# A two-layer trunk: the second layer's output projection as seven half-size products

## The chip, the cores and the metric

The kernel runs on one core of one Trainium2 chip. The metric is the device time of one execution in microseconds (us); each kernel has several timed runs and one profiled execution.

## The reference, cut to what matters

`x` has 512 tokens by 1024 features in float32. The first layer is a pooling mixer, the second a latent attention with 16 heads of 128. Both end in an output projection of 2048 by 1024, and a final norm follows:

```python
def pool_layer(x, norm_g, w_in, w_group, scale, w_out):
    ...
    y = mixed * jax.nn.silu(z)
    return x + y @ w_out

def mla_layer(x, cos, sin, norm_g, w_in, q_norm_g, w_q_b, kv_norm_g, w_kv_b, w_out):
    ...
    o = causal_mla_attention(q_nope, q_rope, k_nope, k_rope, v)
    y = o.reshape(B, S, MLA_WIDTH) * jax.nn.silu(z)
    return x + y @ w_out

def reference(...):
    ...
    return rmsnorm(x, final_norm)
```

## The kernel before

Every float32 matmul is made of three: each operand is split into a high part (float32r, written by ScalarE, ACT) and a low part (the rest, written by VectorE, DVE, or now and then GpSimd, POOL), and `mm3` (L181) issues high x high, low x high and high x low. `strip` (L170) loads a piece of weights through five `raw` buffers and splits it into a pair of `w` tiles, of which four stand (two strips at a time). `halves` (L187) splits an activation. Work is traced in program order; a planner with its own cost model then sets the order of instructions on each engine and inserts the semaphores, but the final block (`finish`) keeps its written order. All plain DMAs go through the queue of SyncE (SP); DMAs that add into SBUF go through POOL's.

The first layer's output projection is done as seven products of half size (L581 to L722). `y` is cut into quarters: `a11` and `a12` are the first 256 tokens with the first and second 1024 of the contraction, `a21` and `a22` the last 256 tokens. Sums of quarters of `y` are made on DVE (`combine`, L628) and split (`split_tokens`, L632). Sums of quarters of the weights are made by DMA: `Summed.load` (L587) loads a quarter into four tiles of 512 KB by SP and then, with `add`, has POOL issue DMAs that add another quarter into the same tiles. `multiply` (L638) is one product: 2 token tiles x 8 contraction tiles x 3 = 48 matmuls of 128x512. `gather` (L657) adds a bank to the residual `xs`.

In the second layer heads run in the loop at L1103. Head h computes the scores of head h+1, transposes head h's probabilities (`transposes`, L1053; DVE writes `pt_lo`), and multiplies by the values (`values`, L1068, which also scales `y`). Heads 0 to 13 cover the softmax's latency with projections of later heads; heads 12 to 15 have blocks of the output projection as fill:

```python
fill = {12: [(0, 0)], 13: [(0, 1)], 14: [(1, 0), (1, 1)], 15: [(2, 0), (2, 1)]}
```

`OutProj` (L529) does this projection in the ordinary way: eight strips of 256 contraction rows, each for four token tiles and two halves of the columns, accumulated in eight banks: 16 x 4 x 2 x 3 = 384 matmuls of 128x512, the last six of them cut into twelve of 128x256. Each strip's weights and two heads of `y` are split on ACT and DVE. 36 matmuls run as fill, the rest after head 15 (L1136 to L1144). `finish` (L1193) does the last strip token tile by token tile, with squares, the power on POOL, the gain and the scaling, and eight output DMAs.

Of the kernel before, what the change touches and what calls it, by code (L numbers as in the profile page):

```python
# [11 lines left out]
F32 = mybir.dt.float32  # L12
# [5 lines left out]
P = 128  # L18
D = 1024
# [31 lines left out]
def trunk_kernel(  # L51
# [477 lines left out]
    class OutProj:  # L529
        def __init__(self, w, apart=None):  # L530
            self.w, self.acc, self.st, self.apart = w, {}, {}, apart

        def load(self, s, tile_of):
            (wv,) = strip([(w_rows(self.w, 2 * s, 2), 2, D)])
            ys = []
            for j in range(2):
                yh, yl = tile_of("h", j), tile_of("l", j)
                halves(y[:, 2 * s + j, :], yh, yl)
                ys.append((yh, yl))
            self.st[s] = (wv, ys)  # L540

        def strip(self, s):
            for j in range(2):
                for t in range(NT):
                    for n in range(2):
                        self.block(s, t, n, j)

        def block(self, s, t, n, j):
            wv, ys = self.st[s]
            if (t, n) not in self.acc:  # L550
                self.acc[t, n] = bank()
            mm3(
                self.acc[t, n],
                tuple(v[:, t * P : (t + 1) * P] for v in ys[j]),
                tuple(v[:, j, n * 512 : (n + 1) * 512] for v in wv),
                s == 0 and j == 0,
                j == 1 and s == (6 if self.apart == (t, n) else 7),
            )

        def columns(self, o, s, t, c):  # L560
            wv, ys = self.st[s]
            for j in range(2):
                mm3(
                    o,
                    tuple(v[:, t * P : (t + 1) * P] for v in ys[j]),
                    tuple(v[:, j, c] for v in wv),
                    j == 0,
                    j == 1,
                )

        def add(self, t, n):
            c = slice(n * 512, (n + 1) * 512)
            return dve.tensor_tensor(xs[:, t, c], self.acc[t, n], xs[:, t, c], ALU.add)

    w_out = pool_w_out[0]
    LEFT, RIGHT = slice(0, 512), slice(512, D)

    class Summed:  # L581


        def __init__(self, tiles):
            self.tiles = tiles
# [677 lines left out]
```

## Time and profile before

| what | value |
|---|---|
| median of 3 runs | 727.72 us (726.13 to 728.48) |
| the profiled execution's own time | 728.38 us |
| its span, first to last instruction | 726.6 us |
| mean granted TensorE clock over the span | 0.992 of full speed |

The span leaves out 1.78 us of the execution's own time. PE is TensorE's matmuls, PEld its weight loads. A matmul's listed duration is longer than its distance to the next one, since matmuls are pipelined: the distance between starts is what counts. Idle time in front of an instruction is shown with what released it.

### The profile page before, as it was taken

The page shows a single profiled execution, that of the slowest core. Times are in us where ns is not written, and L with a number is a line of the kernel's source. Part 1 is how long each engine was busy: PE and PEld are TensorE (multiplying, and loading weights), DVE is VectorE, ACT ScalarE, POOL GpSimd, SP SyncE. Part 2 cuts the span into 40 slices and gives each one's busy share as a digit, 9 for nine tenths or more (in the row PEclk, how much of TensorE's full clock was granted, in tenths as well). Part 3 has the DMA queues.
Part 4 walks back from the last instruction along what each step waited for, and adds up shares of the span by engine and source line. Part 5 has one row for each costly group of instructions (what it writes and reads, how often), then busy time and mean ns, then how long its engine had stood idle before and what let it go on. Part 6 is the DMA issues. An engine that isn't in the chain of part 4 may idle for free.

```text
span 726.6 us, 9988 instructions
## 1 busy us (share of the span) xinstructions
PE 712.1 (98%) x3571; PEld 607.1 (84%) x3571; DVE 417.6 (57%) x834; ACT 337.0 (46%) x739; POOL 116.9 (16%) x159
## 2 busy tenths in 40 slices
PE   7999999999999999999999999999999999999995
PEld 7988888888888887799888888888888988888884
DVE  5964453463577897742724212786876877733325
ACT  6452242242244466545723235575566565533314
POOL 5000000000001350145500023222033100000006
PEclk8999999999999999999999999999999999999998
DMA  8341331332365996135333523132142131113203
GB/s 260 109 142 60 115 115 60 115 112 62 116 189 111 243 179 132 53 109 153 103 102 83 142 74 94 52 81 63 44 113 66 37 96 59 59 59 116 95 7 115
DMA packets 65057, 74.38 MB, mean 102 GB/s; under 512 B 11760, under 2 KB 45680, under 8 KB 65008
## 3 DMA queue, kind: packets, MB, share of 16 engines
q1 hardware_dynamic: 60512, 65.16, 30.1%
q0 software_dynamic: 4352, 8.39, 6.6%
q8 instruction: 28, 0.46, 0.3%
q14 instruction: 21, 0.17, 0.1%
q10 hardware_dynamic: 144, 0.20, 0.1%
HBM read 67.44 MB, written 2.10 MB: 96 GB/s over the span
## 4 chain that ended last, share of the span: by engine, by line
PE 86%; DMA 4%; issue 3%; DVE 3%; POOL 2%; ACT 1%; SPq 0%; POOLq 0%; ACTq 0%
PE bank L185 26%; PE bank L183 26%; PE bank L184 26%; PE bank L1059 2%; PE bank L301 2%; DMA b_y<-in_pool_w_out 2%; PE bank L1022 1%; PE bank L1023 1%; DMA b_x<-in_pool_w_out 1%; POOL b_x L591 1%; DMA raw<-in_pool_w_in 1%; PE bank L1025 1%; PE bank L226 1%; ACT pm L1045 1%; DVE pm L1051 1%
## 5 line engine op out<-in xcount | busy, mean ns | idle before, releaser
L166 ACT ACTIVATE w_hi<-raw 128x512 fp32r<-128x512 f32 (+2 forms) x216 | 114.1, 580 | 153.3 <-PE bank L184 142.3
L167 DVE TENSOR_TENSOR w_lo<-raw,w_hi 128x512 fp32r<-128x512 f32 x148 | 96.8, 690 | 135.6 <-ACT w_hi L166 135.6
L183 PE MATMUL bank<-h_hi,w_hi 128*128 128x512 f32 x368 | 143.4, 390 | 0.0
L185 PE MATMUL bank<-h_lo,w_hi 128*128 128x512 f32 x368 | 143.2, 389 | 0.0
L184 PE MATMUL bank<-h_hi,w_lo 128*128 128x512 f32 x368 | 143.2, 389 | 0.0
L167 POOL TENSOR_TENSOR w_lo<-raw,w_hi 128x256 fp32r<-128x256 f32 (+2 forms) x68 | 61.3, 933 | 193.4 <-ACT w_hi L166 193.3
L185 PEld LDWEIGHTS bank<-h_lo,w_hi 128*128 128x128 f32 x368 | 69.1, 188 | 14.4
L183 PEld LDWEIGHTS bank<-h_hi,w_hi 128*128 128x128 f32 x368 | 69.1, 188 | 14.3
L184 PEld LDWEIGHTS bank<-h_hi,w_lo 128*128 128x128 f32 x368 | 69.1, 188 | 14.2
L185 PE MATMUL bank<-w_lo,h_hi 128*128 128x512 f32 (+1 forms) x176 | 64.2, 365 | 0.4 <-DVE w_lo L608 0.4
L183 PE MATMUL bank<-w_hi,h_hi 128*128 128x512 f32 (+1 forms) x176 | 64.6, 367 | 0.0
L184 PE MATMUL bank<-w_hi,h_lo 128*128 128x512 f32 (+1 forms) x176 | 64.1, 364 | 0.0
L183 PE MATMUL bank<-latT_hi,w_hi 128*128 128x512 f32 x104 | 42.3, 406 | 0.0
L185 PE MATMUL bank<-latT_lo,w_hi 128*128 128x512 f32 x104 | 40.7, 391 | 0.0
L184 PE MATMUL bank<-latT_hi,w_lo 128*128 128x512 f32 x104 | 40.6, 391 | 0.0
L1029 DVE CUSTOM_DVE_ANT_0 pm<-bank,mask 128x128 f32<-128x128 f32 (+2 forms) x64 | 30.6, 489 | 16.0 <-PE bank L185 11.0
L185 PEld LDWEIGHTS bank<-w_lo,h_hi 128*128 128x128 f32 x176 | 33.0, 188 | 5.3 <-DVE w_lo L608 0.8
L183 PEld LDWEIGHTS bank<-w_hi,h_hi 128*128 128x128 f32 x176 | 33.0, 188 | 4.4
L184 PEld LDWEIGHTS bank<-w_hi,h_lo 128*128 128x128 f32 x176 | 33.1, 188 | 4.3
L1045 ACT ACTIVATE pm<-pm,nm 128x128 f32<-128x128 f32 (+1 forms) x64 | 35.3, 557 | 2.4 <-DVE nm L1042 2.0
L188 ACT ACTIVATE pt_hi<-bank 128x512 fp32r<-128x512 f32 (+2 forms) x48 | 20.1, 491 | 23.3 <-PE bank L1059 23.3
L456 POOL MEMSET u<- 128x32 f32 x8 | 1.0, 125 | 178.9 <-DVE sums L468 106.1
(209 smaller groups left out, 1414.5 us busy)
## 6 DMA issues: line engine op xcount, KB each, us to landing
raw<-in_pool_w_in SPq DMA_DIRECT2D x64, 256.0 KB, 3.1
raw<-in_mla_w_in SPq DMA_DIRECT2D x32, 256.0 KB, 3.3
raw<-in_mla_w_out SPq DMA_DIRECT2D x32, 256.0 KB, 3.3
b_x<-in_pool_w_out POOLq DMA_DIRECT2D x12, 512.0 KB, 7.7
raw<-in_mla_w_q_b SPq DMA_DIRECT2D x36, 128.0 KB, 2.5
raw<-in_pool_w_group SPq DMA_DIRECT2D x16, 256.0 KB, 2.7
q_r<-stack SPq DMA_DIRECT2D x64, 64.0 KB, 2.0
raw<-in_mla_w_kv_b SPq DMA_DIRECT2D x16, 256.0 KB, 2.9
```

Of the source, the lines that this page charges most:

```text
L166: act.activation(hi, raw, AF.Copy)
L167: ins = eng.tensor_tensor(lo, raw, f32(hi), ALU.subtract)
L183: pe.matmul(o, a[0], b[0], start=start, stop=False, skip_group_check=more)
L184: pe.matmul(o, a[1], b[0], start=False, stop=False, skip_group_check=more)
L185: pe.matmul(o, a[0], b[1], start=False, stop=stop, skip_group_check=more)
L188: act.activation(hi, src, AF.Copy)
L226: pe.transpose(pt[:, i * P : (i + 1) * P], xn[:, k * P : (k + 1) * P], ident)
L301: pe.matmul(first[i][:, c], w0.views[0][a][:, k, i * P : (i + 1) * P], (h_hi, h_lo)[b][:, k, c], start=k == 0 and n == 0, stop=k == KD - 1 ...
L591: pool.dma_start(t, src, accum_op=ALU.add)
L1029: dve.tensor_tensor_reduce(out=pm[:, OFF[i] : OFF[i] + w], in0=o[:, :w], in1=mask[:, S - w :], scale=1.0, scalar=-3.0e38, op0=ALU.add, op1 ...
L1045: act.activation(v, v, AF.Exp, bias=nm[:, i : i + 1], scale=SCALE, accum_out=l[:, i : i + 1])
L1059: pe.transpose(b[:, n : n + P], pm[:, OFF[i] + j * P : OFF[i] + (j + 1) * P], ident)
```

## The change

The second layer's projection is done by the first layer's seven products, so 7 x 48 = 336 matmuls of 128x512 stand where 384 stood (the last twelve of them are cut into 24 of 128x256). `OutProj` goes away; `Summed`, `combine`, `split_tokens` and `multiply` become functions for both layers, with the first layer's calls and order as before.

The first product (`a11`, heads 0 to 7, with the upper left quarter of the weights) is the fill of heads 12 to 15, twelve matmuls in each. Between the heads stand also: the splits of `a11` (heads 12 and 13), the two strips of its weights, loading and adding the second product's weights (`x_sum`, now eight tiles of 256 KB that take over buffers of queries and keys), the differences `s1` and `s2` of three of the four pieces of `y`, and part of their splits. After head 15 the last piece is made, and the other six products follow. `y_sum` (four tiles of 512 KB) takes over the buffers of the probabilities. `finish` does the seventh product: token tiles 0 and 1 are normed during it, tile 2 behind it, and tile 3's left half is computed in two parts of 256 columns; `normed` multiplies by the row's factor and the gain in one DVE instruction, and the last output halves leave by SP's and ACT's queues.

```diff
...
+        def __init__(self, w, n):
+            self.w, self.n, self.tiles = w, n, []
+        def load(self, half, c, add=False, pieces=None):
+            for i in pieces or range(len(self.tiles)):
+                src = w_rows(self.w, half * 8 + self.n * i, self.n)[:, :, c]
                 if add:
+                    pool.dma_start(self.tiles[i], src, accum_op=ALU.add)
                 else:
+                    nc.sync.dma_start(self.tiles[i], src)
+        def strip(self, i, eng=dve):
             hi = wp.tile([P, W], F32R, name="w_hi", tag="w", bufs=WB)
             lo = wp.tile([P, W], F32R, name="w_lo", tag="w", bufs=WB)
             hv, lv = (t.rearrange("p (k c) -> p k c", k=4) for t in (hi, lo))
+            m = 4 // self.n
+            for j in range(m):
+                k = slice(self.n * j, self.n * (j + 1))
+                raw = self.tiles[m * i + j]
+                act.activation(hv[:, k, :], raw, AF.Copy)
+                eng.tensor_tensor(lv[:, k, :], raw, f32(hv[:, k, :]), ALU.subtract)
+            return hv, lv
+        def strips(self):
+            return [self.strip(i) for i in range(2)]
...
+    def part(o, wv, slot, q, t, start, stop, more, c=whole_row):
+        for k in range(4):
+            mm3(
+                o,
+                tuple(v[:, 4 * q + k, t * P : (t + 1) * P] for v in slot),
+                tuple(v[:, k, c] for v in wv),
+                start and k == 0,
+                stop and k == 3,
+                more=more,
+            )
+    def multiply(banks, strips, slot, start, then=None):
+        for q in range(2):
+            for t in range(2):
+                part(banks[t], strips[q], slot, q, t, start and q == 0, q == 1, not start)
+                if then and q == 1:
+                    then(t)
...
-    o2 = OutProj(mla_w_out[0], apart=(NT - 1, 1))
-    def y_late(half, j):
-        n = "qk"[j] + half
-        return ap.tile([P, S], F32R, name=n, tag=n, bufs=2)
+    w_out2 = mla_w_out[0]
+    a11, a12, a21, a22 = quarters()
+    x_sum, y_sum = Summed(w_out2, 1), Summed(w_out2, 2)
+    def slot_of(hi, lo):
+        return tuple(
+            home.tile([P, 8, 256], F32R, name=name, tag=tag, bufs=1)
+            for name, (home, tag) in (("a_hi", hi), ("a_lo", lo))
+        )
+    def sum_tiles(n):
+        for i in range(n):
+            tag = ("qh", "ql", "kh", "kl")[i]
+            x_sum.tiles.append(ap.tile([P, 1, S], F32, name="b_x", tag=tag, bufs=2))
     (k0, q0), (k1, q1), vs = projections(0)
     qr = {1: QRope(1)}
@@ -1099,13 +1073,22 @@
     for u in vs:
         u()
     units = projections(1)
-    fill = {12: [(0, 0)], 13: [(0, 1)], 14: [(1, 0), (1, 1)], 15: [(2, 0), (2, 1)]}
+    first_half, slots = {}, {}
     for h in range(H):
         p, odd = divmod(h, 2)
         g, t = divmod(h + 5, 4)
-        if h == min(fill):
-            o2.load(0, y_late)
+        if h == 12:
+            slots[1] = slot_of((lp, "t2"), (lp, "q_r"))
+            first_half[0] = columns_of(w_out2, 0, LEFT, 0)
+            split_tokens(a11, slots[1], (0, 1))
+            acc = [bank() for _ in range(2)]
+        if h == 13:
+            split_tokens(a11, slots[1], (2, 3))
         nxt = scores(h + 1) if h + 1 < H else None
+        if h in (13, 14):
+            sum_tiles(4)
+            x_sum.load(0, LEFT, pieces=range(4 * (h - 13), 4 * (h - 12)))
+            x_sum.load(0, RIGHT, add=True, pieces=range(4 * (h - 13), 4 * (h - 12)))
         if odd:
             ahead = projections(p + 2) if p + 2 < H // 2 else [[], [], []]
         transposes(sc[0])
@@ -1115,9 +1098,23 @@
             units[odd][0]()
         if units[odd]:
             units[odd][1]()
-        for i, (t_, n) in enumerate(fill.get(h, ())):
-            for j in range(2):
-                o2.block(0, t_, n, j)
+        if h >= 12:
+            q, t_ = divmod(h - 12, 2)
+            part(acc[t_], first_half[q], slots[1], q, t_, q == 0, q == 1, False)
+        if h == 14:
+            slots[0] = slot_of((lp, "latT_hi"), (wk, "q_r"))
+            s1 = lp.tile([P, 8, 256], F32, name="s1", tag="latT_lo", bufs=1)
+            s1 = [s1[:, 2 * i : 2 * i + 2, :] for i in range(4)]
+            s2 = [
+                lp.tile([P, 2, 256], F32, name="s2", tag=tag, bufs=1)
+                for tag in ("cosT", "sinT", "k_a", "k_b")
+            ]
+            combine(s1, a21, a22, ALU.subtract, range(3))
+            split_tokens(s1, slots[0], range(2))
+        if h == 15:
+            t1 = x_sum.strip(0)
+            split_tokens(s1, slots[0], (2,))
+            combine(s2, s1, a11, ALU.subtract, range(3))
         values(h)
         if g < 4 and t < 2:
             if t == 0:
@@ -1129,96 +1126,135 @@
             for u in units[2]:
                 u()
             units = ahead
+        if h == 13:
+            first_half[1] = columns_of(w_out2, 0, LEFT, 1)
         sc = nxt
+    combine(s1, a21, a22, ALU.subtract, (3,))
+    split_tokens(s1, slots[0], (3,))
+    y_sum.tiles = [
+        ap.tile([P, 2, S], F32, name="b_y", tag=tag, bufs=n)
+        for tag, n in (("pm", 2), ("pm", 2), ("pt_hi", 1), ("pt_lo", 1))
+    ]
+    y_sum.load(1, RIGHT)
+    both = [bank() for _ in range(2)]
+    t1 = [t1, x_sum.strip(1)]
+    x_sum.load(1, RIGHT, add=True)
+    multiply(both, t1, slots[0], True)
+    for t in range(2):
+        gather(t, LEFT, acc[t])
+    combine(s2, s1, a11, ALU.subtract, (3,))
+    split_tokens(s2, slots[1])
+    multiply(acc, x_sum.strips(), slots[1], False)
+    x_sum.load(1, LEFT, add=True)
+    for t in range(2):
+        gather(2 + t, RIGHT, both[t])
+    combine(s2, s2, a12, ALU.add)
+    split_tokens(s2, slots[0])
+    for t in range(2):
+        gather(t, RIGHT, acc[t], ALU.subtract)
+    multiply(both, y_sum.strips(), slots[0], False)
+    y_sum.load(0, RIGHT, add=True)
     g_fin = row(final_norm, D, "g_fin", tag="gain")
-    o2.load(1, y_late)
-    for n in range(2):
-        for j in range(2):
-            o2.block(0, 3, n, j)
-    o2.strip(1)
-    for s in range(2, 8):
-        o2.load(s, y_late)
-        if s < 7:
-            o2.strip(s)
+    s3 = [
+        v.rearrange("p (i k c) -> p i k c", i=2, k=2)[:, i]
+        for v in (xn_tile(), xn_tile())
+        for i in range(2)
+    ]
+    combine(s3, a11, a21, ALU.subtract)
+    split_tokens(s3, slots[1])
+    for t in range(2):
+        gather(t, RIGHT, both[t])
+    multiply(acc, y_sum.strips(), slots[1], False)
+    split_tokens(a12, slots[0])
+    last = [bank() for _ in range(2)]
+    multiply(last, [columns_of(w_out2, 1, LEFT, i) for i in range(2)], slots[0], True)
     o = [
         ap.tile([P, D], F32, name="o", tag=tag, bufs=n)
         for tag, n in (("pm", 2), ("pm", 2), ("pt_hi", 1), ("pt_lo", 1))
     ]
-    junk = lp.tile([P, 512], F32, name="junk", tag="t2", bufs=1)
+    junk = lp.tile([P, 512], F32, name="junk", tag="turned", bufs=1)
     ssq = {t: [] for t in range(NT)}
     rs = {}
...
+    def square(t, c):
         r = sm.tile([P, 1], F32, name="ssq", tag="ssq8", bufs=12)
+        act.activation(
+            junk[:, : c.stop - c.start], xs[:, t, c], AF.Square, scale=D**-0.5, accum_out=r
+        )
         ssq[t].append(r)
     def total(t):
         r = sm.tile([P, 1], F32, name="total")
         pool.tensor_scalar(r, ssq[t][0], EPS, None, ALU.add)
         for q in ssq[t][1:]:
             pool.tensor_tensor(r, r, q, ALU.add)
+        ssq[t] = [r]
+    def power(t):
         rs[t] = sm.tile([P, 1], F32, name="rs")
-        pool.tensor_tensor(rs[t], r, mhalf, ALU.pow)
-    def gained(eng, t, c):
-        eng.tensor_tensor(o[t][:, c], xs[:, t, c], g_fin[:, c], ALU.mult)
-    def scaled(eng, t, c, queue=nc.sync):
-        if eng is act:
-            act.activation(o[t][:, c], o[t][:, c], AF.Copy, scale=rs[t])
-        else:
-            eng.tensor_scalar(o[t][:, c], o[t][:, c], rs[t], None, ALU.mult)
+        pool.tensor_tensor(rs[t], ssq[t][1], ssq[t][0], ALU.add)
+        pool.tensor_tensor(rs[t], rs[t], mhalf, ALU.pow)
+    def send(t, c, queue=nc.sync):
         queue.dma_start(out[0, t * P : (t + 1) * P, c], o[t][:, c])
+    def normed(t, c):
+        dve.scalar_tensor_tensor(
+            o[t][:, c], xs[:, t, c], rs[t], g_fin[:, c], ALU.mult, ALU.mult
+        )
+        send(t, c)
+    def gained(t, c):
+        dve.tensor_tensor(o[t][:, c], xs[:, t, c], g_fin[:, c], ALU.mult)
+    def scaled(t, c, queue=nc.sync):
+        act.activation(o[t][:, c], o[t][:, c], AF.Copy, scale=rs[t])
+        send(t, c, queue)
+    for t in range(2):
+        gather(2 + t, RIGHT, acc[t], ALU.subtract)
+    split_tokens(a22, slots[1])
+    t4 = x_sum.strips()
     def finish():
...
+        for t in range(2):
+            square(t, RIGHT)
+            square(2 + t, RIGHT)
+        for t in range(2):
+            gather(t, LEFT, last[t])
             total(t)
-            if t == 1:
-                scaled(act, 0, lefts)
-                scaled(act, 0, rights)
-        scaled(act, 1, lefts)
-        block(3, 0)
-        o2.add(3, 0)
-        square(3, lefts)
-        gained(pool, 3, lefts)
-        scaled(dve, 1, rights)
-        columns(slice(512, 768))
-        square(3, slice(512, 768))
-        columns(slice(768, D))
-        square(3, slice(768, D), dve)
-        scaled(dve, 2, rights)
-        scaled(act, 2, lefts)
+            square(t, LEFT)
+            power(t)
+        for t in range(2):
+            part(acc[t], t4[0], slots[1], 0, t, False, False, True)
+            for c in (LEFT, RIGHT):
+                normed(t, c)
+        part(acc[0], t4[1], slots[1], 1, 0, False, True, True)
+        gather(2, LEFT, acc[0])
+        total(2)
+        square(2, LEFT)
+        gained(3, RIGHT)
+        c0, c1 = slice(0, 256), slice(256, 512)
+        part(acc[1][:, c0], t4[1], slots[1], 1, 1, False, True, True, c0)
+        power(2)
+        rest = bank()[:, c0]
+        part(rest, t4[1], slots[1], 1, 1, True, True, False, c1)
+        gather(3, LEFT, acc[1])
+        square(3, c0)
         total(3)
-        gained(dve, 3, rights)
-        scaled(dve, 3, slice(0, 640))
-        scaled(act, 3, slice(640, D), act)
+        normed(2, LEFT)
+        gather(3, c1, rest)
+        square(3, c1)
+        power(3)
+        normed(2, RIGHT)
+        scaled(3, RIGHT, act)
+        normed(3, LEFT)
     with tc.manual_schedule():
         finish()
```

## Rows read from the trace of the kernel before

**Rows 1.** The page: busy us (share of the span) and instructions of an engine.

```profile
...
PE 712.1 (98%) x3571; PEld 607.1 (84%) x3571; DVE 417.6 (57%) x834; ACT 337.0 (46%) x739; POOL 116.9 (16%) x159
```

**Rows 2.** Windows: stretch, length, busy us of each engine, PE clock, DMA share, GB/s.

```profile
...
600.00:640.10 40.10, 40.10 (x237) 35.14 (x236) 27.79 (x75) 22.65 (x63) 0.00 (x0) 1.00 0.17 53
640.10:718.50 78.40, 78.35 (x353) 64.92 (x351) 30.92 (x48) 25.92 (x51) 7.96 (x13) 1.00 0.22 71
234.50:311.00 76.50, 75.51 (x340) 62.04 (x340) 61.43 (x79) 43.89 (x62) 22.52 (x22) 1.00 0.72 150
...
234.30:245.20 10.90, 10.90 (x49) 9.01 (x48) 10.86 (x15) 6.33 (x8) 4.85 (x4) 1.00 1.00 259
```

**Rows 3.** Timeline of PE, the projection's end: start, duration, line, operation, operands.

```profile
...
709.38 0.39 PE L183 MATMUL bank<-w_hi,kh 128*128 128x512 f32 x1
...
716.63 0.39 PE L185 MATMUL bank<-w_lo,kh 128*128 128x512 f32 x1
716.86 0.28 PE L183 MATMUL bank<-w_hi,qh 128*128 128x256 f32 x1
...
718.17 0.28 PE L185 MATMUL bank<-w_lo,kh 128*128 128x256 f32 x1
```

**Rows 4.** Timeline of PE in the first layer's fifth product.

```profile
...
279.24 0.40 PE L184 MATMUL bank<-w_hi,h_lo 128*128 128x512 f32 x1
280.04 0.50 PE L185 MATMUL bank<-w_lo,h_hi 128*128 128x512 f32 x1 [0.41 <-DVE w_lo L608]
```

**Rows 5.** Timeline of DVE: splits and sums of pieces, several in a row.

```profile
...
235.70 2.35 DVE L608 TENSOR_TENSOR w_lo<-b_x,w_hi 128x1024 fp32r<-128x1024 f32 x2
...
266.52 1.29 DVE L189 TENSOR_TENSOR h_lo<-s,h_hi 128x512 fp32r<-128x512 f32 x2
...
643.76 2.49 DVE L167 TENSOR_TENSOR w_lo<-raw,w_hi 128x512 fp32r<-128x512 f32 x4
```

**Rows 6.** Timeline of PE and DVE at the last two heads.

```profile
...
634.42 1.18 PE L1059 MATMUL bank<-ident,pm 128*128 128x128 f32 x9
...
638.40 0.39 PE L183 MATMUL bank<-pt_hi,xn 128*128 128x512 f32 x1
...
633.62 1.28 DVE L1051 TENSOR_SCALAR pm<-pm,l 128x128 f32<-128x128 f32 x4
...
636.00 1.49 DVE L189 TENSOR_TENSOR pt_lo<-bank,pt_hi 128x512 fp32r<-128x512 f32 x3 [0.51 <-ACT pt_hi L188]
640.39 0.69 DVE L1082 TENSOR_TENSOR y<-bank,y 128x512 f32<-128x512 f32 x1 [2.90 <-PE bank L1081]
```

**Rows 7.** POOL's adding DMAs, first layer: timeline, tile b_x, queues at 244:254.

```profile
...
242.50 2.43 POOL L591 DMA_DIRECT2D b_x<-in_pool_w_out  x2 [2.62 <-DVE w_lo L608]
...
L591 POOL DMA_DIRECT2D b_x<-in_pool_w_out x12: 1194/1206/1524, 226.8 to 262.2; - x12
...
DMA to landing us min/median/max: 4.4/7.3/10.7
...
q0 software_dynamic: 1062, 2.04, 112.3%
```

**Rows 8.** Timelines of DVE, ACT, POOL in the tail; last, a first-layer norm.

```profile
...
718.87 0.75 DVE L1191 TENSOR_TENSOR xs<-bank,xs 128x256 f32<-128x256 f32 x2
...
719.40 0.42 ACT L1163 ACTIVATE junk<-xs 128x256 f32<-128x256 f32 x1
...
722.29 0.62 ACT L1183 ACTIVATE o<-o,rs 128x384 f32<-128x384 f32 x1 [1.77 <-POOL rs L1176]
...
720.72 0.89 POOL L1174 TENSOR_TENSOR total<-total,ssq 128x1 f32<-128x1 f32 x2
721.69 0.57 POOL L1176 TENSOR_TENSOR rs<-total,mhalf 128x1 f32<-128x1 f32 x1
...
300.93 1.28 DVE L218 SCALAR_TENSOR_TENSOR xn<-xs,rs,g_mla 128x1024 f32<-128x1024 f32 x1 [2.19 <-POOL rs L204]
```

More of the change, by code (lines that the diff above doesn't have):

```diff
@@ L590, in load @@
                 if add:
-                    pool.dma_start(t, src, accum_op=ALU.add)
+                    pool.dma_start(self.tiles[i], src, accum_op=ALU.add)
                 else:
-                    nc.sync.dma_start(t, src)
-        def strips(self):
-            return halves_of(self.tiles)
-    def halves_of(raws, eng=dve):
-        out = []
-        for i in range(2):
+                    nc.sync.dma_start(self.tiles[i], src)
+        def strip(self, i, eng=dve):
             hi = wp.tile([P, W], F32R, name="w_hi", tag="w", bufs=WB)
@@ L604, in halves_of @@
             hv, lv = (t.rearrange("p (k c) -> p k c", k=4) for t in (hi, lo))
-            for j in range(2):
-                k = slice(2 * j, 2 * j + 2)
-                act.activation(hv[:, k, :], raws[2 * i + j], AF.Copy)
-                eng.tensor_tensor(lv[:, k, :], raws[2 * i + j], f32(hv[:, k, :]), ALU.subtract)
-            out.append((hv, lv))
-        return out
-    def columns_of(half, c):
-        return [
-            strip([(w_rows(w_out, half * 8 + 4 * i, 4)[:, :, c], 4, 512)])[0] for i in range(2)
-        ]
@@ new lines, in strip, with columns_of, quarters, combine @@
+            return hv, lv
+        def strips(self):
+            return [self.strip(i) for i in range(2)]
+    def columns_of(w, half, c, i):
+        return strip([(w_rows(w, half * 8 + 4 * i, 4)[:, :, c], 4, 512)])[0]
+    def quarters():
+        return [
+            [
+                y[:, half * 8 + 2 * i : half * 8 + 2 * i + 2, t * 256 : (t + 1) * 256]
+                for i in range(4)
+            ]
+            for t in range(2)
+            for half in range(2)
+        ]
+    def combine(out, a, b, op, pieces=range(4)):
+        for i in pieces:
+            dve.tensor_tensor(out[i], a[i], b[i], op)
@@ new lines, in split_tokens @@
+    def split_tokens(src, slot, pieces=range(4)):
+        for i in pieces:
+            halves(src[i], slot[0][:, 2 * i : 2 * i + 2, :], slot[1][:, 2 * i : 2 * i + 2, :])
+    def part(o, wv, slot, q, t, start, stop, more, c=whole_row):
[8 more added lines that the diff above has]
+            )
@@ L626, in sums @@
         ]
[L628 to L663 removed]
+    w_out = pool_w_out[0]
+    x_sum, y_sum = Summed(w_out, 2), Summed(w_out, 2)
+    x_sum.tiles = [
+        wk.tile([P, 2, PAD + S], F32, name="b_x", tag="t4", bufs=4)[:, :, :S] for _ in range(4)
+    ]
     y_tiles = [wk.tile([P, 4, S], F32, name="b_y", tag=n) for n in ("d_hi", "d_lo")]
[L665 removed]
+    y_sum.tiles = [t[:, 2 * i : 2 * i + 2, :] for t in y_tiles for i in range(2)]
     s1, s3 = sums("s1"), sums("s3")
@@ L689, in trunk_kernel @@
     combine(s1, s1, a12, ALU.add)
-    split_tokens(s1, 0)
-    multiply(both, y_sum.strips(), 0, False)
+    split_tokens(s1, slots[0])
+    multiply(both, y_sum.strips(), slots[0], False)
     y_sum.load(0, RIGHT, add=True)
@@ L700, in trunk_kernel @@
     last = [bank() for _ in range(2)]
-    split_tokens(a12, 0)
-    multiply(last, columns_of(1, LEFT), 0, True)
+    split_tokens(a12, slots[0])
+    multiply(last, [columns_of(w_out, 1, LEFT, i) for i in range(2)], slots[0], True)
     xn = {}
```

142 lines of the change are left out of this document (24 added, 118 removed).

## The prediction

> **What bounds the kernel now.** I read the page's busy times first: matmuls are listed as running for 712.1 of 726.6 us [rows 1]. A listed duration overlaps the next one, so this alone says little; the windows say more. In the stretch of heads 12 to 15 (600.0 to 640.1) and in the whole projection behind it (640.1 to 718.5) PE has no gap worth a name, at the full granted clock, while DVE has 27.79 of 40.1 us and then only 30.92 of 78.4 us of work [rows 2]. The timeline of PE then gives the true price of a matmul: 32 steps from 709.38 to 716.63 are 7.25 us, 0.2266 us for 512 columns; eleven steps from 716.86 to 718.17 give 0.119 us for 256 [rows 3]. So up to T = 718.17 + 0.28 = 718.45 the kernel is a gapless row of matmuls, and only fewer columns make it shorter. Behind T lie 8.15 us of final norm. The first layer, which already does its projection by the seven products, is the model for what else they ask: DVE busy for 61.43 of 76.5 us, for 10.86 of 10.90 in the first of them, DMA at 0.72 of its time [rows 2].
>
> **The matmuls removed.** Before: 378 x 0.2266 + 12 x 0.119 = 87.1 us. After: 324 x 0.2266 + 24 x 0.119 = 76.3 us. That is 10.8 us off an engine that never rests, all of it on the path as long as the next operands are there in time. One product lasts 48 x 0.2266 = 10.9 us. Since the fill of heads 12 to 15 grows from 36 to 48 matmuls, the heads end 2.7 us later (642.8), and the projection behind them is shorter by 13.5.
>
> **What the heads get.** In halves of 512 elements per partition, a DVE operation costs 2.49 / 4 = 0.62 us in a row of four, a sum or an activation's split much the same (1.29 / 2) [rows 5]. The old loads put ten such operations between 600 and 640.1 (eight for weights, two for `y`); the new heads hold up to 25: twelve for three strips, seven splits, six sums. So 15 x 0.62 = 9.3 us are added and DVE stands at 37.1 of 42.8 us, 87%. ACT makes the high part for nine of them (the six sums have none), at some 0.6 us each, on top of 22.65 us of 40.1 [rows 2]: it has room. What hides the DVE work is DVE's idle time, and the question is whether it falls into the gaps. At head 15 it can: `pt_lo` ends at 636.00 + 1.49 = 637.49, the value matmuls that need it start at 638.40 behind the last fill, and DVE then idles 2.90 us before `y` at 640.39 [rows 6]. Cover is therefore 0.9 us on the PE side and 2.9 on DVE's. In heads 12 and 13 the fill doubles, so there the cover grows by 1.4 us each. In head 14 the strip `first_half[1]` must wait for the buffers of the last pair's weights, as the old second strip did, but now it is needed by head 14's own fill; its four pieces of 0.62 us about keep step with PE, which takes 0.68 us (three matmuls) for each. I take 0.5 us of stall for all four heads; bounds 0 and 6 (worked out below).
>
> **Queues.** POOL is idle in the heads (0.00 us) [rows 2], so the eight adding DMAs of the second product's weights wait for nobody but their own plain loads. On SP their loads stand ahead of the raws of `first_half[1]` and later of `y_sum`, `g_fin` and the sixth product's raws. The first four wait for buffers of head 13's scores, long done; the last four wait for head 15's scores, and what stands behind them is not wanted for over 20 us. I cost this at nothing; if the last four came late, the second product's second half would wait, 5.4 us after its start.
>
> **The products behind the heads.** For the third product DVE has eight strip pieces, four splits, four sums and two gathers, 18 x 0.62 = 11.2 us against 10.9 of PE; the fourth and fifth have tiles of twice the width, 2.35 / 2 = 1.18 us for each of four [rows 5], about 10.9 in all; the sixth and seventh have no sums, 8.7. So DVE is filled from about 643 to 676 and a stall of a fraction of a microsecond per product is likely; the first layer ran so with one stall that I can find: in its fifth product two neighbouring matmuls start at 279.24 and 280.04, 0.57 us more than a step, behind `w_lo` of the last summed tiles [rows 4]. Those tiles are late because the adding DMAs fill the DMA engines: in 10 us they moved 2.04 MB at a share of 112.3% [rows 7], 2.57 us for 512 KB. From the first add for the third product (242.50 [rows 7]) to that stall lie 37.5 us, and twelve such adds, 30.8 us, fall into it. The second layer moves the same bytes there as sixteen adds of 256 KB and four of 512; by bytes again 30.8 us, plus at most 1 MB of `y_sum`'s plain loads, whose buffers go free only behind head 15 (5.1 us at the same rate): 35.9 of 37.5. POOL's issue takes 1.21 us for 512 KB [rows 7]; for 256 KB I bound it by half and by the same, eight of them 4.8 to 9.7 us, within a product. I take 1.5 us of stall for the six products, bounds 0 and 4.
>
> While many adds are in flight, 512 KB cost 2.57 us, though each takes 4.4 to 10.7 us from issue to landing [rows 7]. The Trainium skill, "DMA: Bandwidth & Descriptors", section "Anatomy of one DMA", gives a DMA issued by GpSimd a fixed cost of about 2 us beside its bytes; an estimate by it is 2.6 us for each 256 KB, and eight in a row, if nothing overlapped, 20.8 us per product, which would make the change a loss. By that page the 512 KB adds would take 3.2 us each; the trace's 2.57 is less, so the fixed part overlaps. No run here shows an add of 256 KB.
>
> **The tail.** Before, the last row factor is ready at 721.69 + 0.57 = 722.26, 3.81 us behind T, and from there to the span's end it is 4.34 us (scaling, issue, landing). After, the last chain from T: a wait for DVE, which may still be in `normed(2, LEFT)` (between 0.05 and 0.7 us, half of the 1.28 us norm in the first layer; I take 0.3), the gather of 256 columns 0.4, the square 0.42 and some 0.1 for its sum, one addition on POOL 0.45 and the power 0.57 [rows 8], in all 2.25; then 4.34, and 0.1 more because each queue now gets 512 columns after a 0.7 us operation instead of 640 and 384. That is T + 6.7, 1.4 us less than 8.15. Best case 1.8. The gathers of tiles 0 and 1 may queue on DVE behind the seventh product's last strip, which cannot be split before the sixth product frees its buffers; that could cost up to 1 of the 1.4.
>
> **The sum.** The profiled execution took 728.38 us: 728.38 - 10.8 - 1.4 + 0.5 + 1.5 = 718.2. It lies 0.66 us above the median of the runs, so against the median of 727.72 this is 717.5 us.
>
> **Rivals.**
> *Nothing stalls.* Stalls 0 and the tail at 1.8: 728.38 - 0.66 - 10.8 - 1.8 = 715.1. For it: the first layer's single 0.57 us. Against it: the DVE load of 87% and then 100%. Chance 0.06.
> *The last heads become DVE-bound.* If the eight operations of head 15 (5.0 us) are placed ahead of `pt_lo`, PE waits 5.0 - 0.9 = 4.1 us, and the three additional ones of head 14 (1.9 us) ahead of the softmax delay the last transposes as much: 6.0 instead of 0.5, 723.0 us. For it: in-order queues, 15 more operations, and a chain scores, softmax, transposes, values with 0.9 us of slack. Against it: the gaps are there, and the planner knows the priority of the heads. Chance 0.22, with a range of 720 to 725.
> *Slower: an add costs the same at half the size.* If a 256 KB add holds the DMA engines 2.57 us, twenty adds and the plain loads take 56.5 us where 37.5 are to be had: the fifth product waits 19 us instead of 1, 735.5 us. It decides from about 2.1 us per add, where 16 x 0.8 us of excess eats the gain. For it: nothing in the trace has such an add. Against it: rows of 2 KB per partition stay as they are, and engines at full share are limited by bytes. By the fixed cost of the page named above, in the Trainium skill, small adds would be dear in the same way; that the 512 KB adds overlap speaks against it. Chance 0.09, of which a third ends within the error.
> The forecast has 0.63, with a range of its own of 715.5 to 720.
>
> **Numbers.** What a measurement of this kernel can tell from no change is about 0.3%, 2.2 us. Faster by more: the forecast, the first two rivals, 0.91 less a little for heads and products both at their worst, 0.90. Within: 0.04. Slower: 0.06. For the range, 715.0 to 723.5 leaves out a part of the no-stall case (0.03), the far end of the heads' case (0.05) and the small adds (0.09).
>
> **What would show it.** Right: the steps of 0.2266 us go on through heads and products; DVE in heads 12 to 15 near 37 us; the last matmul near 709.6 us of the span; the last row factor 2.3 us behind it. Wrong at the heads: PE idle in front of the transposes or values of head 15, released by `pm` or `pt_lo`. Wrong at the products: PE idle at their first or third quarter, released by `w_lo` of the summed tiles, and ACT waiting for the DMAs of `b_x` or `b_y`. Wrong at the tail: DVE still at `normed(1)` when tile 2's bank is ready. What would make the whole prediction wrong is an order in which sums for a later product stand ahead of what the next matmul needs.

## The result and the profile after

| | before | after |
|---|---|---|
| median (lowest to highest), 4 runs each | 727.54 us (726.13 to 728.48) | 721.23 us (719.77 to 722.07) |
| profiled execution, span, clock | 728.38, 726.6, 0.992 | 719.77, 717.9, 0.997 |

The ratio is 0.9913, 95% interval 0.9889 to 0.9936: 6.3 us faster, where 10.2 were forecast, and inside the range (715.0 to 723.5). The median lies above the range that the forecast had for itself (715.5 to 720).

The profiled execution of after was 1.8 us ahead of that of before already at head 11, which the change does not touch: the last value matmuls of that head start at 595.09 against 596.89. So stretches are compared from that point. From there to the end of the last matmul before takes 121.56 us and after 115.68; from the last matmul's end to the span's end 8.15 and 7.13.

The page's busy times, answering to [rows 1] (busy us, share, instructions):

```profile
PE 701.2 (98%) x3529; PEld 597.8 (83%) x3529; DVE 450.9 (63%) x883; ACT 353.6 (49%) x765; POOL 137.4 (19%) x182
```

Windows, in the columns of [rows 2]: the heads, the turn to the products, the third and the fourth product.

```profile
600.00:642.80 42.80, 41.75 (x239) 36.37 (x238) 33.96 (x85) 25.29 (x68) 10.70 (x12) 1.00 0.68 172
640.00:644.00 4.00, 2.95 (x15) 2.47 (x15) 2.97 (x6) 1.55 (x4) 0.82 (x1) 1.00 1.10 238
644.00:648.00 4.00, 4.00 (x19) 3.32 (x18) 1.40 (x4) 3.47 (x7) 1.79 (x3) 1.00 1.10 266
653.40:666.20 12.80, 11.17 (x48) 8.94 (x48) 12.11 (x20) 7.80 (x11) 7.10 (x8) 1.00 1.06 181
```

In the heads DVE has 33.96 of 42.8 us. Then, between 640 and 648, it has only 4.37 of 8, while the DMA engines are over 1.0, and in the window from 653.4 to 666.2 it has 12.11 of 12.8 and PE falls to 11.17. The timeline of PE, with the idle time ahead of an instruction and its releaser in brackets, shows four waits, where before had none (PE is gapless in [rows 2]); the last row is the last matmul.

```profile
641.06 0.49 PE L1044 MATMUL bank<-pt,v 128*128 128x128 f32 x2 [1.05 <-ACT pt L1029]
...
653.44 0.50 PE L185 MATMUL bank<-w_lo,a_hi 128*128 128x512 f32 x1 [0.51 <-DVE w_lo L560]
...
666.27 0.50 PE L185 MATMUL bank<-w_lo,a_hi 128*128 128x512 f32 x1 [1.67 <-DVE w_lo L560]
...
678.14 0.50 PE L185 MATMUL bank<-w_lo,a_hi 128*128 128x512 f32 x1 [0.67 <-DVE w_lo L560]
...
710.49 0.28 PE L185 MATMUL bank<-w_lo,a_hi 128*128 128x256 f32 x1
```

They stand at head 15's values and in the third, fourth and fifth product. ACT and DVE show what lies behind the first two. ACT's timeline:

```profile
639.70 1.15 ACT L559 ACTIVATE w_hi<-b_x 128x512 fp32r<-128x512 f32 x2 [1.20 <-DMA b_x<-in_mla_w_out]
640.75 0.26 ACT L1029 ACTIVATE pt<-bank 128x128 f32<-128x128 f32 x1
...
644.53 0.63 ACT L559 ACTIVATE w_hi<-b_x 128x512 fp32r<-128x512 f32 x1 [2.98 <-DMA b_x<-in_mla_w_out]
645.07 2.18 ACT L188 ACTIVATE a_hi<-s 128x512 fp32r<-128x512 f32 x4
...
654.37 0.64 ACT L559 ACTIVATE w_hi<-b_x 128x512 fp32r<-128x512 f32 x1 [0.99 <-DMA b_x<-in_mla_w_out]
655.82 0.63 ACT L559 ACTIVATE w_hi<-b_x 128x512 fp32r<-128x512 f32 x1 [0.82 <-DMA b_x<-in_mla_w_out]
657.11 0.63 ACT L559 ACTIVATE w_hi<-b_x 128x512 fp32r<-128x512 f32 x1 [0.66 <-DMA b_x<-in_mla_w_out]
```

DVE's timeline:

```profile
641.59 0.69 DVE L1045 TENSOR_TENSOR y<-bank,y 128x512 f32<-128x512 f32 x1 [1.03 <-PE bank L1044]
...
647.28 0.69 DVE L189 TENSOR_TENSOR a_lo<-s,a_hi 128x512 fp32r<-128x512 f32 x1 [2.60 <-ACT a_hi L188]
...
657.78 0.69 DVE L560 TENSOR_TENSOR w_lo<-b_x,w_hi 128x512 fp32r<-128x512 f32 x1 [0.60 <-ACT w_hi L559]
...
659.58 2.49 DVE L583 TENSOR_TENSOR s<-s,y 128x512 f32<-128x512 f32 x4
661.99 2.50 DVE L189 TENSOR_TENSOR a_lo<-s,a_hi 128x512 fp32r<-128x512 f32 x4
...
665.00 1.22 DVE L560 TENSOR_TENSOR w_lo<-b_y,w_hi 128x1024 fp32r<-128x1024 f32 x1
```

At 639.70 ACT works on `w_hi` of `b_x`, a tile of the second product's weights, for which it has waited 1.20 us; `pt`, which head 15's values need, stands behind it in ACT's order. At 644.53 it has waited 2.98 us for the next tile, with four splits of `s1` and `s2` behind it (`a_hi`, 645.07); DVE idles 1.03 and 2.60 us, the second time for the first of those `a_hi`. From 647.28 to 666.2 DVE then idles only 0.60 us, and the fourth product starts when its `w_lo<-b_y` of 665.00 is done: behind the third product's last tile (657.78) stand gathers, the four sums and four splits of the fourth product.

POOL's timeline shows when the adds of the late tiles are issued:

```profile
631.80 0.86 POOL L546 DMA_DIRECT2D b_x<-in_mla_w_out  x1 [20.31 <-DVE nm L1005]
633.31 6.18 POOL L546 DMA_DIRECT2D b_x<-in_mla_w_out  x7 [0.66 <-DMA b_x<-in_mla_w_out]
```

and the DMA view of 629 to 650 (issues, KB each, median us to landing) how long they take:

```profile
b_x<-in_mla_w_out POOLq DMA_DIRECT2D x12, 256.0 KB, 9.1
b_y<-in_mla_w_out SPq DMA_DIRECT2D x4, 512.0 KB, 9.9
```

The eight of 631.80 to 639.5 are the last four of the second product and the first four of the third, mixed in POOL's order. An add takes 9.1 us to land (median), beside the plain loads of `y_sum` with 9.9. From these issues until the last tile of the third product has landed the DMA engines are full (share 1.05), in a window with the columns of [rows 2]:

```profile
631.00:657.00 26.00, 24.45 (x118) 20.09 (x117) 22.22 (x42) 13.33 (x30) 13.59 (x18) 1.00 1.05 235
```

The tail, in the timeline of all engines, answering to [rows 8]:

```profile
711.13 0.41 DVE L610 TENSOR_TENSOR xs<-xs,bank 128x256 f32<-128x256 f32 x1
...
711.64 0.42 ACT L1184 ACTIVATE junk<-xs 128x256 f32<-128x256 f32 x1 [0.97 <-DVE xs L610]
...
712.56 0.57 POOL L1201 TENSOR_TENSOR rs<-rs,mhalf 128x1 f32<-128x1 f32 x1
713.16 0.72 ACT L1216 ACTIVATE o<-o,rs 128x512 f32<-128x512 f32 x1 [1.01 <-POOL rs L1201]
713.16 0.75 DVE L1207 SCALAR_TENSOR_TENSOR o<-xs,rs,g_fin 128x512 f32<-128x512 f32 x1 [0.95 <-POOL rs L1201]
713.91 0.40 ACTq L1204 DMA_DIRECT2D out<-o  x1
```

With T = 710.49 + 0.28 = 710.77, the last row factor is ready at 713.13, T + 2.36, and the span ends 4.77 us later.

### The profile page after: what moved, and what is told of

Its sections match the earlier page's. It is cut to its first block, busy times and chain, and to the rows that moved or that the text cites. A ratio compares the mean times of both kernels' runs of the same rounds, so it can differ in the third digit from the quotient of the medians.

```text
span 717.9 us, 10034 instructions
## 1 busy us (share of the span) xinstructions
PE 701.2 (98%) x3529; PEld 597.8 (83%) x3529; DVE 450.9 (63%) x883; ACT 353.6 (49%) x765; POOL 137.4 (19%) x182
## 4 chain that ended last, share of the span: by engine, by line
PE 87%; DVE 5%; DMA 4%; ACT 2%; issue 1%; POOL 1%; POOLq 0%; SPq 0%; ACTq 0%
PE bank L185 26%; PE bank L184 26%; PE bank L183 26%; DMA b_x<-in_mla_w_out 3%; PE bank L1022 2%; PE bank L301 2%; PE bank L985 2%; PE bank L986 1%; DMA b_y<-in_mla_w_out 1%; DVE a_lo L189 1%; PE bank L988 1%; PE bank L226 1%; ACT pm L1008 1%; DVE pm L1014 1%; DVE w_lo L560 1%
## 5 line engine op out<-in xcount | busy, mean ns | idle before, releaser
L166 ACT ACTIVATE w_hi<-raw 128x512 fp32r<-128x512 f32 (+2 forms) x200 | 105.0, 576 | 130.0 <-PE bank L184 119.7
L167 DVE TENSOR_TENSOR w_lo<-raw,w_hi 128x512 fp32r<-128x512 f32 x132 | 86.6, 691 | 114.0 <-ACT w_hi L166 114.0
L185 PE MATMUL bank<-w_lo,a_hi 128*128 128x512 f32 (+1 forms) x116 | 44.7, 386 | 2.8 <-DVE w_lo L560 2.8
L183 PE MATMUL bank<-w_hi,a_hi 128*128 128x512 f32 (+1 forms) x116 | 44.6, 385 | 0.0
L184 PE MATMUL bank<-w_hi,a_lo 128*128 128x512 f32 (+1 forms) x116 | 44.5, 383 | 0.0
L559 ACT ACTIVATE w_hi<-b_x 128x512 fp32r<-128x512 f32 (+1 forms) x40 | 30.6, 798 | 24.8 <-DMA b_x<-in_mla_w_out 9.3
L560 DVE TENSOR_TENSOR w_lo<-b_x,w_hi 128x512 fp32r<-128x512 f32 (+1 forms) x40 | 34.3, 902 | 6.1 <-ACT w_hi L559 5.9
```

The lines of the kernel that those rows point to most:

```text
L166: act.activation(hi, raw, AF.Copy)
L167: ins = eng.tensor_tensor(lo, raw, f32(hi), ALU.subtract)
L183: pe.matmul(o, a[0], b[0], start=start, stop=False, skip_group_check=more)
L184: pe.matmul(o, a[1], b[0], start=False, stop=False, skip_group_check=more)
L185: pe.matmul(o, a[0], b[1], start=False, stop=stop, skip_group_check=more)
L559: act.activation(hv[:, k, :], raw, AF.Copy)
```

## The experiments

Each is measured by the stretch from head 11's last value matmuls to the end of the last matmul: before 121.56, after 115.68; before less the 10.8 us of matmuls is 110.8. (Where a quote says 115.4 for after, it counts to the start of the last matmul.) Each quote names theories of its own. All but run 10 are single executions; the stretch leaves out the spread in what lies ahead of head 11, up to 2.1 us from one profile to the next. Runs 4 and 8 change next to nothing of the stretch and give 115.53 and 115.54 beside after's 115.68, so two or three tenths of a microsecond tell nothing.

**1. The softmax's copy first.** The second strip's pieces on ACT are queued behind head 15's `pt` copy.

```diff
-                act.activation(pt_3, b[:, n:], AF.Copy)
+                copied.append(act.activation(pt_3, b[:, n:], AF.Copy).ins)
...
-    t1 = [t1, x_sum.strip(1)]
+    with tc.issue_after(copied[-1]):
+        t1 = [t1, x_sum.strip(1)]
```

> The four weight pieces of the second product's second strip are issued on ACT behind head 15's copy of pt_3, nothing else changes. Theory 1 (ACT stands in order at a piece whose adding DMA has not landed, and the copy that head 15's last value matmul needs is behind it): the 1.05 us that PE waits for the copy goes, the time from head 11's last value matmul to the last matmul falls from 115.4 to about 114.2 us, the product stalls (3.3 us in three places) stay within 0.5. Theory 2 (DVE is simply full, as the rival of the prediction had it): PE waits about as long in the same place for something DVE writes, 115.0 or more.

Measured: 720.43 us, stretch 116.35. Head 15's wait is gone, and the time is not: the products wait for more, which neither theory had. PE's timeline:

```profile
647.79 0.50 PE L184 MATMUL bank<-w_hi,a_lo 128*128 128x512 f32 x1 [0.23 <-DVE a_lo L189]
...
653.20 0.50 PE L185 MATMUL bank<-w_lo,a_hi 128*128 128x512 f32 x1 [0.80 <-DVE w_lo L560]
...
666.98 0.50 PE L185 MATMUL bank<-w_lo,a_hi 128*128 128x512 f32 x1 [2.61 <-DVE w_lo L560]
```

The wait at head 15 was a symptom; what sets the date of the fourth product lies elsewhere.

**2. No adds.** The 28 adding DMAs of the second layer are left out, so its weight sums are not made.

```diff
-            x_sum.load(0, RIGHT, add=True, pieces=range(4 * (h - 13), 4 * (h - 12)))
...
-    x_sum.load(1, RIGHT, add=True)
...
-    x_sum.load(1, LEFT, add=True)
...
-    y_sum.load(0, RIGHT, add=True)
```

> All 28 adding DMAs of the second layer are left out, so the products use single quarters of the weights instead of their sums; every matmul, split and sum on DVE stays. Theory 1 (late adding DMAs on full DMA engines hold up ACT, and DVE falls behind): PE waits under 1 us in heads and products together, 115.4 falls to about 111.5. Theory 2 (DVE has 11.2 us of work per product of 10.9): head 15's wait goes, but the product stalls stay at 2.5 us or more, about 114.

Measured: 715.36 us, stretch 110.64, no wait of PE at all. DVE's work is the same as in after, so a full DVE alone does not make the stalls. (The load of the DMA engines falls too, so this does not tell late adds from full DMA engines.)

**3. No sums of tokens.** The sums `s2`, `s2` + `a12` and `s3` on DVE are left out; other quarters are split in their place.

```diff
-            combine(s2, s1, a11, ALU.subtract, range(3))
...
-    combine(s2, s1, a11, ALU.subtract, (3,))
-    split_tokens(s2, slots[1])
+    split_tokens(s1, slots[1])
...
-    combine(s2, s2, a12, ALU.add)
-    split_tokens(s2, slots[0])
+    split_tokens(s1, slots[0])
...
-    combine(s3, a11, a21, ALU.subtract)
-    split_tokens(s3, slots[1])
+    split_tokens(a21, slots[1])
```

> Twelve DVE sums of y are left out (s2, its second sum, and s3), so products three to five use other operands than they should; all DMAs, splits and matmuls stay. Theory 1: head 15's wait for the copy stays (1 us), the wait in the third product stays, together 1.5 to 3 us. Theory 2: with 7.4 us less on DVE the product stalls go (under 0.5 us of 3.3), 115.4 falls to about 112.

Measured: 716.17 us, stretch 112.29. Head 15's wait stays (1.44 us), all waits of the products are gone, as theory 2 had it. So late transfers alone do not make those either: it takes both, late tiles and the work that DVE has behind them.

**4. Other adds later.** The adds for the last products' tiles (second half of the contraction, left columns) are issued behind those of `y_sum`.

```diff
-    x_sum.load(1, LEFT, add=True)
...
     y_sum.load(0, RIGHT, add=True)
+    x_sum.load(1, LEFT, add=True)
```

> The eight adds that only the seventh product needs are issued behind the four adds of the fifth product instead of before them. Theory 1: the fifth product's tiles land up to 10 us earlier and its stall (0.8 us) goes, the third's and fourth's stay; about 114.6. Theory 2: no difference beyond 0.3 us, 115.4.

Measured: 720.67 us, stretch 115.53, waits of 0.71, 0.65, 1.77 and 0.56 us: no difference. These adds were not what made the others late.

**5. Splits into the gap.** Three of the four splits of `s2` come right behind head 15's `pt` copy, the second strip's pieces behind them.

```diff
+    with tc.issue_after(marks[-1]):
+        early = split_tokens(s2, slots[1], range(3))
     combine(s1, a21, a22, ALU.subtract, (3,))
-    split_tokens(s1, slots[0], (3,))
+    late = split_tokens(s1, slots[0], (3,))
...
-    t1 = [t1, x_sum.strip(1)]
+    t1 = [t1, x_sum.strip(1, behind=(early, early, early, late))]
...
```

> Edit: three of the third product's four token splits stand right behind head 15's softmax copy on ACT, and the second strip's last four tiles behind them, so that DVE has work in the 2.6 and 1.0 us that it stood idle around 641 to 647. No transfer changes. Theory A (DVE is behind by what it idled there, and PE pays for it in products 3 to 5, 3.3 us): from head 11's last value matmuls to the last matmul's end 112.5 to 113.5 instead of 115.7, time 717.5 to 719. Rival B (the late transfers alone set the dates, at any order): 115 to 116, the stalls only stand elsewhere.

Measured: 720.11 us, stretch 115.95, which is rival B's range. Theory A missed, for a reason that DVE's timeline shows: the gap was filled, and a gap as long opened where the third product's tiles were waited for.

```profile
640.95 1.88 DVE L189 TENSOR_TENSOR a_lo<-s,a_hi 128x512 fp32r<-128x512 f32 x3
...
652.53 0.69 DVE L189 TENSOR_TENSOR a_lo<-s,a_hi 128x512 fp32r<-128x512 f32 x1 [3.08 <-ACT a_hi L188]
...
659.77 2.49 DVE L585 TENSOR_TENSOR s<-s,y 128x512 f32<-128x512 f32 x4
662.17 2.49 DVE L189 TENSOR_TENSOR a_lo<-s,a_hi 128x512 fp32r<-128x512 f32 x4
```

The sums of the fourth product still stand behind the last of these tiles (659.77), so DVE's date for the fourth product did not move. DVE's idle time between 641 and 647 was therefore not what the fourth product waits for. What did not move either is the date of that last tile, in ACT's timeline:

```profile
657.30 0.63 ACT L561 ACTIVATE w_hi<-b_x 128x512 fp32r<-128x512 f32 x1 [0.67 <-DMA b_x<-in_mla_w_out]
```

In after ACT takes it up at 657.11. Its add is issued at 646.91 in this run and at 649.11 in after: issued 2.2 us earlier, it lands no earlier.

**6. Earlier tiles.** Two of the second product's tiles get buffers that are free at head 13, so that none of its adds waits for head 15's scores. (Two pieces of `s2` take other buffers for it.)

```diff
-            sum_tiles(4)
+            if h == 13:
+                sum_tiles(*((ap, tag, 2) for tag in ("qh", "ql", "kh", "kl")))
+                sum_tiles((lp, "cosT", 1), (lp, "sinT", 1))
+            else:
+                sum_tiles((ap, "qh", 2), (ap, "ql", 2))
+            now = range(6) if h == 13 else range(6, 8)
...
```

> Edit: two of the last four weight tiles of the second product get other buffers and are loaded and added at head 13, the last two at head 14, so that none of the eight adds waits for head 15's scores. Theory A (the late adds leave ACT waiting 3 us and DVE idle 3.6 us): ACT's wait of 2.98 us before the second strip falls under 1, head 15's wait of 1.05 goes, and the stretch from head 11 is 112.5 to 113.5. Rival B (the DMA engines are full, so that other transfers are late instead): ACT waits for y_sum or the third product's tiles, and the stretch stays over 114.5.

Measured: 716.78 us, stretch 112.69: 3.0 us less than after. Its windows, and behind them the two waits that PE's timeline still has:

```profile
640.00:644.00 4.00, 4.00 (x20) 3.29 (x20) 4.00 (x7) 2.91 (x6) 1.63 (x3) 1.00 1.07 255
644.00:648.00 4.00, 4.00 (x19) 3.34 (x18) 4.00 (x8) 2.48 (x5) 1.86 (x3) 1.00 1.08 311
```

```profile
663.30 0.50 PE L185 MATMUL bank<-w_lo,a_hi 128*128 128x512 f32 x1 [0.82 <-DVE w_lo L560]
...
675.12 0.50 PE L185 MATMUL bank<-w_lo,a_hi 128*128 128x512 f32 x1 [0.63 <-DVE w_lo L560]
```

DVE has 8.00 of 8 us between 640 and 648, where it had 4.37; head 15's wait and the third product's are gone. The DMA engines are as full as before in these windows (1.07 and 1.08). What moved are two 256 KB adds, which POOL now issues at 571.72 and 573.07 and not between 632 and 639, and with them the third product's last tile, which no edit touches. The timelines of ACT and DVE:

```profile
654.15 0.63 ACT L559 ACTIVATE w_hi<-b_x 128x512 fp32r<-128x512 f32 x1 [0.66 <-DMA b_x<-in_mla_w_out]
...
662.03 1.21 DVE L560 TENSOR_TENSOR w_lo<-b_y,w_hi 128x1024 fp32r<-128x1024 f32 x1
```

ACT takes that tile up at 654.15, 3.0 us earlier than in after (657.11), and the fourth product's first `w_lo` comes 7.9 us behind it, as in after (665.00) and in runs 1, 4, 5 and 8: two gathers, four sums, four splits and a gather stand between on DVE. In all six profiles the stretch ends 53.4 to 53.7 us behind that date, whatever DVE or PE waited for earlier. So the late last tile of the third product and the work behind it on DVE make the time of after. That the tile comes earlier here fits transfers that stand in line in full DMA engines: two adds and two loads fewer are ahead of it.

**7. Sums on POOL.** The fourth product's sums go to POOL, with the order of run 4.

```diff
-    combine(s2, s2, a12, ALU.add)
+    combine(s2, s2, a12, ALU.add, eng=pool)
...
```

> Edit: the four token sums of the fourth product are made on POOL and not on DVE, and the adds of its last tiles are issued behind those of y. Theory A (DVE is full through products 3 to 5): 2.5 us less DVE work ahead of the fourth product, its wait of 1.7 falls under 0.5, the stretch from head 11 is 113.5 to 114.5. Rival B (transfers set the date of the fourth product's tiles): 115 to 116. Rival C (POOL's sums delay its own issues of adds): the fifth product waits longer than its 0.7.

Measured: 722.86 us, stretch 117.34, slower than after. The waits of the fourth and fifth product are gone, as A had it, but PE waits 3.42 us at 657.74 in the third, which no theory had. The timelines of POOL and PE, and between them three DVE instructions, each from a view of its own:

```profile
652.20 6.62 POOL L583 TENSOR_TENSOR s<-s,y 128x512 f32<-128x512 f32 x4 [1.15 <-DVE a_lo L189]
...
652.57 1.78 DVE L189 TENSOR_TENSOR a_lo<-s,a_hi 128x512 fp32r<-128x512 f32 x1
...
654.27 1.75 DVE L189 TENSOR_TENSOR a_lo<-s,a_hi 128x512 fp32r<-128x512 f32 x1
...
655.94 1.74 DVE L560 TENSOR_TENSOR w_lo<-b_x,w_hi 128x512 fp32r<-128x512 f32 x1
...
657.74 0.80 PE L185 MATMUL bank<-w_lo,a_hi 128*128 128x512 f32 x1 [3.42 <-DVE w_lo L560]
```

POOL takes 1.65 us for a sum. While it makes them, DVE is at the third product's own splits and first tiles, and these three instructions last 1.74 to 1.78 us instead of 0.68, each until about 0.55 us behind the end of a sum. That accounts for 3.2 of the 3.42 us: beside POOL's sums DVE lost more than it had been relieved of.

**8. The cut undone.** Tile 3's left half as one piece of 512 columns.

```diff
-        c0, c1 = slice(0, 256), slice(256, 512)
-        part(acc[1][:, c0], t4[1], slots[1], 1, 1, False, True, True, c0)
+        part(acc[1], t4[1], slots[1], 1, 1, False, True, True)
...
-        gather(3, c1, rest)
-        square(3, c1)
+        gather(3, LEFT, acc[1])
+        square(3, LEFT)
```

> Edit: the last quarter of the last product stays one piece of 512 columns, the new cut of the last bank undone. Everything ahead is as before. If the cut brings what the rows say (gather .69 instead of .41, square .63 instead of .42, 0.14 less of matmuls): from the last matmul's end to the end 0.35 to 0.5 us more than 7.13. Rival: the row factor is set by the additions on POOL and not by the last gather: under 0.1 more.

Measured: from the last matmul's end to the span's end 7.76 us, 0.63 more than 7.13 and more than the 0.35 to 0.5 expected; the row factor is ready 2.99 behind T instead of 2.36. The longer gather and square account for 0.49; the rest is that the whole gather also waits for DVE, which is scaling the tile before until 713.05. With the 0.14 of matmuls that it costs, the cut is worth 0.49 us. (The stretch is 115.54, 0.14 below after's. Its waits stand elsewhere, though: 0.56 us at head 15 instead of 1.05, and 2.58 in the fourth product instead of 1.67.)

**9. Sums first.** On top of run 6, DVE makes the fourth product's sums between the third product's two strips.

```diff
+    t1 = x_sum.strip(0)
+    with tc.issue_after(x_sum.done):
+        summed = combine(s2, s2, a12, ALU.add)
+    with tc.issue_after(summed):
+        t1 = [t1, x_sum.strip(1)]
-    multiply(acc, x_sum.strips(), slots[1], False)
+    multiply(acc, t1, slots[1], False)
...
-    combine(s2, s2, a12, ALU.add)
```

> Edit: the early tiles of the run before, and DVE makes the four sums for the fourth product between the third product's first and second strip, where it then stood idle 1.5 us waiting for tiles; 8.2 us of DVE work behind the last tile become 5.8. Theory A (what is left of the stalls is DVE's order behind a late transfer): the fourth product's wait of 0.82 goes, the fifth's 0.63 stays; from head 11's last value matmuls to the last matmul's end 111.6 to 112.0 instead of 112.7. Rival B (the tiles of the fourth product land late): the wait stays, 112.7.

Measured: 716.18 us, stretch 110.91, no wait of PE. A was too careful: the fifth product's wait went too. The strips of the fourth product come earlier, so POOL issues the first add of the fifth product's weights 22.0 us behind the start of head 15's last value matmuls and not 24.0, and ACT's wait for them is 0.55 instead of 1.31 us.

**10. Splits first.** On top of run 9, ACT makes the high parts of `s3` ahead of the tiles of the same product.

```diff
-    split_tokens(s3, slots[1])
+    ahead = split_tokens(s3, slots[1])
...
-    multiply(acc, y_sum.strips(), slots[1], False)
+    with tc.issue_after(ahead):
+        t1 = y_sum.strips()
+    multiply(acc, t1, slots[1], False)
```

> Edit: as the run before it, and ACT makes the high parts of the fifth product's four sums ahead of that product's first weight tile, for whose transfer it waited 1.31 us with three of them behind it. Theory A (ACT's order behind a transfer): the fifth product's wait falls under 0.3, the stretch from head 11 is 110.9 to 111.6 (gapless 110.7), the time 714.5 to 717. Rival B (the transfer itself is late for the fifth product): the wait stays, 111.6 to 112.

Measured: 715.43 us (714.52 to 716.41, 5 runs) against 727.61 of before: ratio 0.9835, interval 0.9821 to 0.9848, where after has 0.9913. The stretch is 110.66, gapless; the 0.25 us to run 9, itself without a wait, tell nothing. It beats both kernels. Its window over the third and fourth product:

```profile
653.40:666.20 12.80, 12.80 (x58) 10.59 (x57) 12.26 (x18) 6.74 (x9) 6.60 (x8) 1.00 1.04 175
```

**11. The orders alone.** Runs 9 and 10 without the earlier tiles; the diff is theirs.

> Edit: the two orders alone, without the early tiles. Theory A (the late tiles leave ACT waiting and DVE idle, DVE is then full): head 15's wait of 1 us stays, the fourth product's 1.7 stays over 1 since DVE has only 0.6 us of idle time left to fill, the stretch is 114.5 to 115.7. Rival C (the order of the sums alone is at fault): 112.5 to 113.5.

Measured: 719.32 us, stretch 113.80, between the ranges of A and C: 1.9 us less than after. The fourth product's wait, which A kept over 1, fell to 0.75, and the third's and fifth's shrank too. PE's timeline:

```profile
642.75 0.49 PE L1047 MATMUL bank<-pt,v 128*128 128x128 f32 x2 [1.22 <-ACT pt L1032]
...
654.83 0.50 PE L185 MATMUL bank<-w_lo,a_hi 128*128 128x512 f32 x1 [0.21 <-DVE w_lo L561]
...
666.78 0.50 PE L185 MATMUL bank<-w_lo,a_hi 128*128 128x512 f32 x1 [0.75 <-DVE w_lo L561]
```

So the two remedies about add: the earlier tiles alone 3.0, the orders alone 1.9, both 5.0 (115.68 to 110.66).

## Why the prediction came out as it did

**The matmuls**: right. Between gapless kernels the stretch falls from 121.56 to 110.66, 10.9 us against 10.8.

**The heads**: the load was less than feared, DVE 33.96 of 42.8 us (34.97 with the earlier tiles of run 6) instead of 37.1, and the rival of DVE-bound heads (723.0) is refuted: no value matmul waits for `pt_lo`. The wait that came, 1.2 us against 0.5, came by ACT: from head 11's value matmuls to head 15's it is 45.97 us in after, 44.77 with the earlier tiles.

**The queues**: this step failed. The prediction saw that the last four tiles wait for the scores of head 15, cost it at nothing, and thought that a late tile would hold only the second half of the second product. What waited for such a tile first was not PE but ACT, which has `pt` and splits of `s1` and `s2` behind it. And the late adds stand in DMA engines that are full until 657, ahead of the third product's tiles: the last of those comes 3.0 us later than in run 6, and 7.9 us pass behind it, nearly all of them DVE's work, before the fourth product's first `w_lo`. Run 6 prices the step at 3.0 us. The wait at head 15, 1.2 us of the stretch in after, is not a price of its own: with it gone (run 1), or half as long (run 8), the fourth product waits for more.

**The products behind**: 1.5 us of stall were taken, and 2.0 are left when the tiles are early (112.69 against 110.66), by `w_lo` of summed tiles as the prediction said in its signs. But not because the DMA engines have no more time: with the sums ahead of the third product's tiles the same transfers are in time. The sum 728.38 - 10.8 - 1.4 + 0.5 + 1.5 becomes 728.38 - 10.9 - 1.0 + 1.2 + 3.8 = 721.5; the profile of after, 1.8 us ahead at head 11, has 719.77.

**The tail**: 1.0 us instead of 1.4. The row factor came at T + 2.36 as forecast (2.25). What was mis-sized is the way from there to the end, 4.77 us where 4.44 were taken: the scaling takes 0.75 us, not 0.62, and from the last issue to the span's end lie 3.99 us, not 3.66.

**The range** held in part by luck: the time fell where the rival of DVE-bound heads had its range (720 to 725), by a mechanism that is not that rival's and that the sum had at nothing.

**Nothing stalls** (715.1) did not happen, but run 10 is that case, at 715.43. **Small adds** are refuted: in after ACT, waiting for the DMA each time, gets the third product's last tiles 1.45 and 1.29 us apart (654.37, 655.82, 657.11), and half of 2.57 is 1.29. The prediction's estimate of 2.6 us for each, from the fixed cost in the Trainium skill, "DMA: Bandwidth & Descriptors", section "Anatomy of one DMA", would hold only if nothing overlapped; the trace shows that adds in flight overlap.

## What to carry to other kernels

An in-order engine that waits for a transfer holds all that is planned behind it: look at what stands behind the first instruction that touches a late tile, on ACT as well as on PE, and put what is ready ahead of it. An idle time of a full engine need not be the price: run 5 filled DVE's and gained nothing. Find the tile that lands last, count the work planned between it and the next matmul, and shorten that, or take transfers out of the line ahead of the tile. Removing one visible wait proves little until the whole stretch is shorter.

## What the runs showed of the hardware

POOL's issue of an add of 256 KB takes 0.86 us where one of 512 KB takes 1.2, and they land one every 1.29 to 1.45 us with four or five in flight (ACT's rows from 654.37 on), though each takes 7.9 us (median) to land. Plain loads of 512 KB issued among them take 9.9 us (median), and as long as those are under way the adds land some 2 us apart (ACT takes up tiles at 648.58, 650.58 and 652.74). POOL's sum of 128x512 takes 1.65 us in run 7 against DVE's 0.62 in after, and three DVE instructions beside these sums take 1.74 to 1.78 us instead of 0.68.
